# Retention's outputs and state updates issued in pairs: both halves of a pair behind the turn of y, two state steps per call

## The chip, the cores and the metric

The kernel runs on one core of a Trainium2 chip. The metric is the device time of one execution in microseconds. The kernel before took 1388.43 us, the median of three runs (1386.64 to 1389.92).

## What is computed

One layer of a diffusion backbone over 1024 latent tokens and 256 context tokens of width 1024: a modulated RMS norm, one input projection whose columns feed two mixers (bidirectional chunkwise retention with 4 heads, differential attention with 4 heads), an output projection with a gated residual, then a gated MLP with a width 3 convolution, a second residual and a final norm. The change touches retention alone, which the reference states as

```python
    def step(S, inp):
        qc, kc, vc = inp
        scores = jnp.einsum('bhid,bhjd->bhij', qc, kc) * intra
        o = (jnp.einsum('bhij,bhje->bhie', scores, vc)
             + jnp.einsum('bhid,bhde->bhie', qc * q_dec[..., None], S))
        S = S * c_dec[:, None, None] + jnp.einsum('bhjd,bhje->bhde', kc * k_dec[..., None], vc)
        return S, o
...
    for d in range(2):
        def orient(t):
            return jnp.flip(t, axis=2) if d == 1 else t
...
        o_c, s_c = retention_chunked(qc, kc, vc, log_gamma[d], s0)
        o_l, _ = retention_chunked(ql, kl, vl, log_gamma[d], s_c)
        ret_lat = ret_lat + head_group_norm(orient(o_l), gn_g[d])
...
    y_ret_lat = jax.nn.silu(rg_l) * ret_lat.astype(dtype)
```

Chunks have 128 tokens, so a head has 8 chunks of latent tokens and 2 of context, walked forward (d = 0) and backward (d = 1); each chunk's output needs the state S that has come to it from its side.

## The kernel before

The large products are written in three passes: each float32 operand is split into a high part and a remainder, both in the type fp32r, and `passes` (L128 to L133) issues high by high, high by low, low by high. On TensorE that is an endless stream of 128x512 matmuls with lines L131, L132 and L133. Retention's own products are 128x128 in plain float32 and are issued **between** these passes; the trace shows each of them as two MATMUL instructions.

The mixing is done by generators. `natural` and `transposed` (the projections) call `tick` after every k, that is after three passes, and `tick` adds a rate to a counter and calls `next` on the generator that stands beside the projection whenever the counter reaches 1. So a `yield` in the generator is a place where the stream of passes goes on, and what is written between two yields is issued as one group.

Two generators matter. `states((0, 1))` stands beside the projection of block 3 (rate 21/62): it forms the states of heads 0 and 1. A head takes 10 steps, `one` in the code, forward and backward in turn. One step loads k and v of two chunks (`kvs`, 4 buffers, loaded four steps ahead), scales k by its decay on ScalarE (`ks`, L314, 2 buffers, one step ahead), multiplies on TensorE into the PSUM tile `pu` (L330; one or two products) and folds `pu` into the state on VectorE (`S`, L336 and L338). `outputs()` stands beside blocks 0 and 4 (rate 1.35). It walks over 16 pairs of chunks, four of each head. Iteration n loads pair n + 2, scores pair n + 1 (`pc` on TensorE, L254; `sc` on VectorE, L256; `qq` on GpSimd, L251), computes the two halves of pair n's output (`po`, L262 and L263: for each half two directions of scores times v plus q times S), copies and squares it on ScalarE (`o`, `jk`, `ss`), normalises pair n - 1 on VectorE (`o`, L278) and gates it on GpSimd (`y`, L280 and L281), and turns y of pair n - 3 for the output projection (`pyt` on TensorE, L286; `yr` on ScalarE and VectorE; a DMA to `yrd`). An iteration has six yields. In iterations 4 to 11 it also advances the states of heads 2 and 3, five steps in every two iterations.

All small PSUM tiles (`pu`, `pc`, `po`, `pyt`) are taken in the order of the program from one cycle of five banks, `tr_tile`: a tile waits until the tile five places before it has been read.

A scheduler then fixes the order of each engine's instructions; an engine works strictly in that order. Weights of the next block come along with it: `split_slice` (L182) issues a DMA to `raw` on the SyncE queue, casts `whi` on ScalarE (L187) and subtracts `wlo` on VectorE (L188). Block 4's slices pass through the middle of the retention stage. The SyncE queue carries these loads, the loads of k, v and gate (`kvs`, `kvo`) and the stores of `yrd` in one order; a `kvo` load waits until GpSimd has multiplied an earlier pair's y by its gate. At the end, pair 15's y releases GpSimd's loads for attention, `ks` and `qhl` among them, and the first attention scores `pA` (L873) wait for these.

## Time and profile before

| | us |
|---|---|
| median of the three runs | 1388.43 |
| the profiled execution's own time | 1387.15 |
| its span, first to last instruction | 1385.4 |
| TensorE busy in the span | 1363.2 (98%) |
| states of heads 0 and 1 beside block 3 | 273.4 to 318.6 |
| outputs, and states of heads 2 and 3, beside blocks 0 and 4 | about 331 to 428.8 |
| first attention score | 452.2 |

Times in the traces count from the first instruction. The stage that the change touches is thus some 155 us of the span. In rows of the timeline the columns are: start in us, duration in us, engine, line, operation, out<-in, shapes, count of merged instructions, and in brackets the idle time before it and who ended that. A merged row of two matmuls gives the start of the first.

### The profile page before, as it was taken

Reading aid. Unit: us, or ns where it says so; the run is one execution under the profiler, and the core shown is the slowest. Engines: PE = TensorE matmul, PEld = TensorE weight load, DVE = VectorE, ACT = ScalarE, POOL = GpSimd, SP = SyncE. Lnnn points to the kernel's source line nnn. Section 1 sums busy time; section 2 is a strip of 40 time slices with the busy share of each in tenths; the row PEclk is TensorE's granted clock in tenths of the full one; section 3 lists DMA queues with packets and bytes.
Section 4 is the critical chain, followed back from the end, with each engine's and each line's share of the span. In section 5 each row is a group of like instructions: output and inputs, shape, how many; then the busy total and the mean of one; then the engine's idle time right before and its main releaser. Section 6 shows DMA issues by size and latency. Waiting matters only on the chain. (4 is left out here: it accounts for less than half of the span.)

```text
span 1385.4 us, 19442 instructions
## 1 busy us (share of the span) xinstructions
PE 1363.2 (98%) x7042; PEld 1146.0 (83%) x7042; DVE 994.4 (72%) x1469; ACT 732.2 (53%) x1395; POOL 303.6 (22%) x323
## 2 busy tenths in 40 slices
PE   8999999999999999999999999999999999999997
PEld 6788888888988799998888788888888888888886
DVE  4655773424676898895458997788778877798757
ACT  4652322434675789987136654555545555454543
POOL 1310000002655424411200643222332220000001
PEclk9999999999999999999999999999999999999999
DMA  9546885454565778622410232332323325963523
GB/s 373 202 168 210 296 267 184 145 176 144 155 188 151 208 179 182 139 48 99 172 65 23 99 115 99 114 114 94 112 101 112 113 71 174 373 227 106 175 92 129
DMA packets 94759, 214.61 MB, mean 155 GB/s; under 512 B 9220, under 2 KB 29188, under 8 KB 94152
## 3 DMA queue, kind: packets, MB, share of 16 engines
q1 hardware_dynamic: 85928, 186.90, 39.2%
q0 software_dynamic: 8160, 24.91, 7.9%
q10 hardware_dynamic: 576, 1.57, 0.3%
q8 instruction: 55, 0.90, 0.3%
q14 instruction: 40, 0.33, 0.1%
HBM read 158.03 MB, written 55.31 MB: 154 GB/s over the span
## 5 line engine op out<-in xcount | busy, mean ns | idle before, releaser
L131 PE MATMUL pl<-hT,whi 128*128 128x512 f32 x256 | 105.8, 413 | 0.0
L131 PE MATMUL chain<-T,whi 128*128 128x512 f32 x264 | 103.0, 391 | 1.2 <-ACT ub L1298 0.9
L132 PE MATMUL chain<-T,whi 128*128 128x512 f32 x264 | 102.8, 389 | 0.0
L133 PE MATMUL chain<-T,wlo 128*128 128x512 f32 x264 | 102.4, 389 | 0.0
L133 PE MATMUL pl<-hT,wlo 128*128 128x512 f32 x256 | 100.2, 391 | 0.0
L132 PE MATMUL pl<-hT,whi 128*128 128x512 f32 x256 | 99.9, 390 | 0.0
L876 DVE TENSOR_REDUCE mt<-pA 128x1 f32<-128x1280 f32 x64 | 95.1, 1489 | 3.0 <-PE pA L873 1.3
L873 PE MATMUL pA<-ks,qhl 128*128 128x512 f32 (+1 forms) x384 | 89.5, 369 | 1.4 <-DMA ks<-dk 1.0
L131 PE MATMUL c<-whi,ghl 128*128 128x512 f32 x232 | 90.2, 389 | 0.0
L132 PE MATMUL c<-wlo,ghl 128*128 128x512 f32 x232 | 90.2, 389 | 0.0
L133 PE MATMUL c<-whi,ghl 128*128 128x512 f32 x232 | 90.2, 389 | 0.0
L880 ACT ACTIVATE p<-pA,mt 128x1280 f32<-128x1280 f32 x64 | 85.5, 1336 | 5.5 <-DVE mt L876 5.4
L1044 ACT CAST whi<-cmb 128x512 fp32r<-128x512 f32 x62 | 38.5, 623 | 80.5 <-PE chain L132 66.3
L873 PEld LDWEIGHTS pA<-ks,qhl 128*128 128x128 f32 x384 | 67.7, 189 | 13.8 <-issue 1.4
L905 PE MATMUL pv<-va,aT 128*128 128x128 f32 x640 | 77.0, 275 | 0.1
L1204 POOL TENSOR_TENSOR cmb<-wrb 128x512 f32<-128x512 f32 x19 | 28.3, 1488 | 221.1 <-DMA wrb<-w_up 168.2
L1047 DVE TENSOR_TENSOR wlo<-cmb,whi 128x512 fp32r<-128x512 f32 x62 | 60.0, 970 | 20.4 <-ACT whi L1044 20.4
L905 PEld LDWEIGHTS pv<-va,aT 128*128 128x128 f32 x640 | 73.9, 192 | 0.7 <-DVE yT L934 0.3
L1044 ACT CAST whi<-wra 128x512 fp32r<-128x512 f32 x55 | 33.9, 623 | 72.9 <-PE third L132 42.3
L133 PE MATMUL third<-yT,wlo 128*128 128x512 f32 x168 | 65.4, 389 | 0.0
L132 PE MATMUL third<-yT,whi 128*128 128x512 f32 x168 | 65.4, 389 | 0.0
L131 PE MATMUL third<-yT,whi 128*128 128x512 f32 x168 | 65.4, 389 | 0.0
(327 smaller groups left out, 3843.0 us busy)
## 6 DMA issues: line engine op xcount, KB each, us to landing
wm<-w_mod SPq DMA_DIRECT2D x32, 512.0 KB, 5.1
raw<-w_in SPq DMA_DIRECT2D x27, 512.0 KB, 4.7
wra<-w_up SPq DMA_DIRECT2D x24, 512.0 KB, 3.3
wrb<-w_up SPq DMA_DIRECT2D x22, 512.0 KB, 3.5
W<-w_down SPq DMA_DIRECT2D x44, 256.0 KB, 5.8
ad<-s SPq DMA_DIRECT2D x20, 512.0 KB, 3.6
wra<-ad SPq DMA_DIRECT2D x20, 512.0 KB, 3.7
kvs<-kvg SPq DMA_DIRECT2D x36, 256.0 KB, 3.1
```

What stands on the lines that cost most here:

```text
L131: mm(ps, lh, rh, start=first, stop=False, skip_group_check=more)
L132: mm(ps, lh, rl, start=False, stop=False, skip_group_check=more)
L133: return mm(ps, ll, rh, start=False, stop=last, skip_group_check=more)
L873: mm(self.pa[m][:, c0:c1], self.q[:, m, i, qs], self.k[:, m, c0:c1], start=(i == 0), stop=(i == 1))
L876: nc.vector.tensor_reduce(out=self.mt[:, m : m + 1], in_=self.pa[m][:, :LK], axis=AX.X, op=ALU.min)
L880: nc.scalar.activation(self.p[m], self.pa[m][:, :LK], AF.Exp, scale=-1.0, bias=self.mt[:, m : m + 1], accum_out=self.s[:, m : m + 1])
L905: mm(self.pv, self.aT[:, c, :], self.v[:, c, :], start=(c == 0), stop=(c == NKT - 1))
L1044: cast = nc.scalar.copy(hi, src)
L1047: nc.vector.tensor_tensor(out=lo, in0=src, in1=r32(hi), op=ALU.subtract)
L1204: nc.gpsimd.tensor_tensor(out=s1, in0=b1, in1=b2, op=ALU.add)
```

## The change

- A call of `states` now makes two steps, a forward and a backward one. Two scaled keys are held ahead instead of one, and both are made again behind the second product. The rate beside block 3 goes from 21/62 to 11/62, since there are 11 calls instead of 21.
- In `outputs`, the first half of pair n's output moves from its own yield to the place where y is turned and the second half is made: turn, both halves, squares.
- In iterations 4 to 11 the state generator is called once with the scores, and once more in the middle of iterations 4 and 8. That is again 20 steps by the end of iteration 11.

Nothing is added or removed: each engine has as many instructions, and the SyncE and GpSimd queues as many DMAs. Only their order moves.

```diff
@@ -316,15 +316,13 @@
 
             load_until(4)
             yield
-            ahead = scaled_keys(0)
+            ahead = [scaled_keys(0), scaled_keys(1)]
             for i, (h, d, g, cs) in enumerate(seq):
                 if i % len(one) == 0:
                     states_at[h] = [rt.tile([P, NT, P], F32, name=f"S{e}") for e in range(2)]
                     last, made = [None, None], [-2, -2]
                 load_until(i + 4)
-                kv, ks = kvs[i], ahead
-                if i + 1 < len(seq):
-                    ahead = scaled_keys(i + 1)
+                kv, ks = kvs[i], ahead.pop(0)
                 pu = tr_tile([P, 2, P], "pu")
                 for c in cs:
                     mm(pu[:, c, :], ks[:, c, :], kv[:, 1, c, :], start=True, stop=True)
@@ -337,7 +335,9 @@
                     else:
                         nc.vector.scalar_tensor_tensor(out=dst, in0=last[d], scalar=cd[:, d * H + h : d * H + h + 1], in1=pu[:, c, :], op0=ALU.mult, op1=ALU.add)
                     last[d] = dst
-                yield
+                if i % 2:
+                    ahead += [scaled_keys(j) for j in range(i + 1, min(i + 3, len(seq)))]
+                    yield
 
         def outputs():
             n_pairs, per_head = H * NT // 2, NT // 2
@@ -350,13 +350,13 @@
                 if n + 1 < n_pairs:
                     pairs[n + 1].score()
                 forming = per_head <= n < 3 * per_head
-                if n == per_head - 1 or forming and n % 2 == 0:
+                if n == per_head - 1:
+                    next(more)
+                if forming:
                     next(more)
                 yield
-                if 0 <= n < n_pairs:
-                    pairs[n].output(0)
                 yield
-                if forming:
+                if forming and n % per_head == 0:
                     next(more)
                 yield
                 if n == n_pairs + 2:
@@ -366,13 +366,12 @@
                 elif n >= 3:
                     pairs[n - 3].turn()
                 if 0 <= n < n_pairs:
+                    pairs[n].output(0)
                     pairs[n].output(1)
                     pairs[n].squares()
                 yield
                 if 0 <= n - 1 < n_pairs:
                     pairs[n - 1].gate()
-                if forming:
-                    next(more)
                 yield
                 yield
 
@@ -838,7 +837,7 @@
         tr2 = psb2.enter_context(tc.tile_pool(name="tr2", bufs=2, space=PSUM))
         mm2 = psb2.enter_context(tc.tile_pool(name="mm2", bufs=1, space=PSUM))
         banks.update(mm=itertools.cycle([ps_a, ps_a, mm2]), tr=itertools.cycle([pst] * 3 + [tr2] * 2))
-        beside(states((0, 1)), 21 / 62, 0.7)
+        beside(states((0, 1)), 11 / 62, 0.35)
         natural(wg, lat_lhs, range(NT), store_to(kvg_row(2), func=AF.Silu, c0=NTC))
         wg = stream_block(0)
         beside(outputs(), 1.35, -16.0)
```

What the scheduler made of it is seen at three places. The first is TensorE in iteration 5, from the scores of pair 6 to those of pair 7 (`pc`); `pl` are the passes of the projection. Before:

```order
L254 MATMUL pc_3266<-xa,rk 128x128 x2
L262 MATMUL po<-kvo,sc 128x128
L263 MATMUL po<-S_2656,qq 128x128
L262 MATMUL po<-kvo,sc 128x128
L263 MATMUL po<-S_2657,qq 128x128
L131 MATMUL pl<-hT_168,whi 128x512
L132 MATMUL pl<-hT_170,whi 128x512
L133 MATMUL pl<-hT_168,wlo 128x512
L330 MATMUL pu<-kvs,ks 128x128 x2
L131 MATMUL pl<-hT_168,whi 128x512
L132 MATMUL pl<-hT_170,whi 128x512
L133 MATMUL pl<-hT_168,wlo 128x512
```

```order
L286 MATMUL pyt<-ident,y 128x128 x2
L262 MATMUL po<-kvo,sc 128x128
L263 MATMUL po<-S_2656,qq 128x128
L262 MATMUL po<-kvo,sc 128x128
L263 MATMUL po<-S_2657,qq 128x128
L131 MATMUL pl<-hT_168,whi 128x512
L132 MATMUL pl<-hT_170,whi 128x512
L133 MATMUL pl<-hT_168,wlo 128x512
L330 MATMUL pu<-kvs,ks 128x128 x2
```

(The second fence goes on where the first ends, and three more passes end the iteration.) The same iteration of the changed kernel:

```order
L254 MATMUL pc_3277<-xa,rk 128x128 x2
L328 MATMUL pu<-kvs,ks 128x128 x4
L131 MATMUL pl<-hT_168,whi 128x512
L132 MATMUL pl<-hT_170,whi 128x512
L133 MATMUL pl<-hT_168,wlo 128x512
L131 MATMUL pl<-hT_168,whi 128x512
L132 MATMUL pl<-hT_170,whi 128x512
L133 MATMUL pl<-hT_168,wlo 128x512
L286 MATMUL pyt<-ident,y 128x128 x2
L262 MATMUL po<-kvo,sc 128x128
L263 MATMUL po<-S_2670,qq 128x128
L262 MATMUL po<-kvo,sc 128x128
```

(Six more `po` products and six passes follow.) Four groups with three passes behind each have become two groups with six. Over the whole stage, from the first `pu` to the last `pyt`, the row counts give 76 groups before and 47 now. Before, 35 of them have three passes behind them, 16 have six and 24 have nine or more (one has two); now it is 1, 24 and 22.

The second place is where block 4's last weight slice arrives, in iterations 10 and 11. On ScalarE before, from the turn of pair 7's y (`yr`) on; the first `o` is the copy of pair 10's output:

```order
L290 CAST yr<-pyt 128x256
L429 ACTIVATE xb<-pl 64x512
L267 COPY o<-po 128x512
L187 CAST whi<-raw 128x1024
L271 ACTIVATE jk,ss<-o 128x128
L314 ACTIVATE ks<-kvs,kd 128x256
```

and now:

```order
L290 CAST yr<-pyt 128x256
L428 ACTIVATE xb<-pl 64x512
L187 CAST whi<-raw 128x1024
L267 COPY o<-po 128x512
L271 ACTIVATE jk,ss<-o 128x128 x4
```

The cast of the slice now stands ahead of the copy of pair 10's output. On VectorE at the same place, before (`S` are the state updates, `sc` the scores of pair 12):

```order
L432 TENSOR_TENSOR xb<-xb,rtab_2072 128x512
L338 SCALAR_TENSOR_TENSOR S_3516<-S_3516,cd,pu 128x128
L433 TENSOR_TENSOR xa<-xa,xb 128x512
L188 TENSOR_TENSOR wlo<-raw,whi 128x1024
L338 SCALAR_TENSOR_TENSOR S_3516<-S_3516,cd,pu 128x128
L256 TENSOR_TENSOR sc<-pc_3797,dec 128x512
```

and now:

```order
L336 SCALAR_TENSOR_TENSOR S_3518<-S_3518,cd,pu 128x128
L278 SCALAR_TENSOR_TENSOR o<-o,ss,gn 128x128
L291 TENSOR_TENSOR yr<-pyt,yr 128x256
L430 SCALAR_TENSOR_TENSOR xa<-pl,rtab_2072 128x512
L431 TENSOR_TENSOR xb<-xb,rtab_2072 128x512
L188 TENSOR_TENSOR wlo<-raw,whi 128x1024
L432 TENSOR_TENSOR xa<-xa,xb 128x512
L278 SCALAR_TENSOR_TENSOR o<-o,ss,gn 128x128 x3
L256 TENSOR_TENSOR sc<-pc_3799,dec 128x512
```

The state updates of steps 16 and 17 now all stand ahead of the slice's `wlo`; before, one stood behind it.

The third place is GpSimd a little earlier, where pair 8's y (`y`, two rows) and pair 11's scaled queries (`qq`) meet. Before:

```order
L273 TENSOR_TENSOR ss<-ss,mhalf 128x4
L280 TENSOR_TENSOR y<-o 128x256
L251 TENSOR_TENSOR qq<-xa,qd 128x512
L281 TENSOR_TENSOR y<-y,kvo 128x256
L273 TENSOR_TENSOR ss<-ss,mhalf 128x4
```

and now:

```order
L273 TENSOR_TENSOR ss<-ss,mhalf 128x4
L251 TENSOR_TENSOR qq<-xa,qd 128x512
L280 TENSOR_TENSOR y<-o 128x256
L281 TENSOR_TENSOR y<-y,kvo 128x256
L273 TENSOR_TENSOR ss<-ss,mhalf 128x4
```

The queries of pair 11 no longer split pair 8's y but go ahead of it. The load of `kvo` on the SyncE queue that waits for this y stands directly ahead of the last slice's `raw` load now; before, a `kvs` load stood between them.

## The prediction

> **What bounds the kernel now.** I read the page's head first, then the busy times of the two stretches that hold retention, then TensorE's timeline in them, then what TensorE waits for there.
>
> ```profile
> span 1385.4 us, 19442 instructions
> PE 1363.2 (98%) x7042; PEld 1146.0 (83%) x7042; DVE 994.4 (72%) x1469; ACT 732.2 (53%) x1395; POOL 303.6 (22%) x323
> ...
> 273.40:318.60 45.20, 45.20 (x236) 38.39 (x235) 13.25 (x37) 17.21 (x31) 0.00 (x0) 1.00 0.63 187
> 331.00:428.80 97.80, 97.19 (x634) 86.94 (x634) 66.45 (x152) 60.77 (x196) 58.15 (x56) 1.00 0.45 141
> ```
>
> The last two rows give, for each stretch, its length and then the busy time of TensorE, its weight loads, VectorE, ScalarE and GpSimd, the granted clock, the DMA share and GB/s. TensorE is busy for all of the first stretch and for 97.19 of 97.80 us of the second, at the full clock, while VectorE reaches 68% and the others less. So TensorE sets the end, and the change can save only two things there: what a small group costs beyond its own products, and the 0.6 us and more in which TensorE waits. The products themselves all stay.
>
> **What a group costs beyond its products.** First the pace of each kind alone, by the starts.
>
> ```profile
> 268.75 0.39 PE L133 MATMUL pn<-whi,hT 128*128 128x512 f32 x1
> ...
> 271.70 0.39 PE L131 MATMUL pn<-whi,hT 128*128 128x512 f32 x1
> ...
> 336.97 0.38 PE L262 MATMUL po<-kvo,sc 128*128 128x128 f32 x2
> ...
> 337.64 0.39 PE L263 MATMUL po<-S,qq 128*128 128x128 f32 x2
> 337.78 0.47 PE L131 MATMUL pl<-hT,whi 128*128 128x512 f32 x1
> ```
>
> Between the first two rows lie 13 passes in 2.95 us, 0.227 us each. Between the next two lie six small instructions in 0.67 us, 0.112 each. Now whole cycles, from one group to the next:
>
> ```profile
> 276.89 0.61 PE L330 MATMUL pu<-kvs,ks 128*128 128x128 f32 x4
> 277.25 0.48 PE L131 MATMUL pn<-whi,hT 128*128 128x512 f32 x1
> ...
> 279.41 0.61 PE L330 MATMUL pu<-kvs,ks 128*128 128x128 f32 x4
> ...
> 339.25 0.60 PE L254 MATMUL pc<-xa,rk 128*128 128x128 f32 x4
> ...
> 340.39 0.38 PE L262 MATMUL po<-kvo,sc 128*128 128x128 f32 x2
> ```
>
> From 276.89 to 279.41, 2.52 us, stand four small instructions and nine passes: 4 x 0.112 + 9 x 0.227 = 2.49, so 0.03 us is over. From 336.97 to 339.25, 2.28 us, stand eight and six: 0.89 + 1.36 = 2.25, again 0.03 (0.025 with one digit more). From 339.25 to 340.39, 1.14 us, stand four and three: 0.45 + 0.68 = 1.13, so 0.012. A group of four costs no less than one of eight; what counts is that there is a group, and the surplus is spread over the passes behind it. With 0.012, 0.025 and 0.031 for three, six and nine or more passes, the groups before cost 35 x 0.012 + 16 x 0.025 + 24 x 0.031 = 1.56 us, and those now 1 x 0.012 + 24 x 0.025 + 22 x 0.031 = 1.29 us. **The first term is 0.27 us less.** Merging cannot give more than the whole 1.56.
>
> **The two waits.** These are the only waits of TensorE over 0.25 us between the first `pu` group and the last output.
>
> ```profile
> 405.94 0.39 PE L263 MATMUL po<-S,qq 128*128 128x128 f32 x2
> 406.93 0.46 PE L330 MATMUL pu<-kvs,ks 128*128 128x128 f32 x2 [0.60 <-ACT jk L271]
> 407.14 0.47 PE L131 MATMUL pl<-hT,whi 128*128 128x512 f32 x1
> ...
> 410.19 0.39 PE L262 MATMUL po<-kvo,sc 128*128 128x128 f32 x2
> 410.59 0.49 PE L263 MATMUL po<-S,qq 128*128 128x128 f32 x2
> 410.83 0.48 PE L131 MATMUL pl<-hT,whi 128*128 128x512 f32 x1
> ...
> 401.01 0.59 ACT L267 COPY o<-po 128x512 f32<-128x512 f32 x1
> 404.18 1.05 ACT L187 CAST whi<-raw 128x1024 fp32r<-128x1024 f32 x1 [2.58 <-DMA raw<-w_in]
> ...
> 405.36 1.21 DVE L188 TENSOR_TENSOR wlo<-raw,whi 128x1024 fp32r<-128x1024 f32 x1
> 406.49 0.34 DVE L338 SCALAR_TENSOR_TENSOR S<-S,cd,pu 128x128 f32<-128x128 f32 x1
> ...
> 410.19 0.34 DVE L338 SCALAR_TENSOR_TENSOR S<-S,cd,pu 128x128 f32<-128x128 f32 x1
> ```
>
> A row of two small ones takes 0.22 us to the next small one and 0.14 to a pass (337.64 to 337.78). From 405.94 to the pass at 407.14 are 1.20 us where 0.36 would do: 0.84 lost. From 410.19 to 410.83 are 0.64 where 0.36 would do: 0.28 lost. The profile names a ScalarE square for the first, but `pu` of step 19 takes the PSUM bank of step 17's `pu`, five places back, and the last read of that is the state update that ends at 406.83, 0.1 us ahead of the product. It stands behind `wlo`, which waits for `whi`, which waits for the slice's DMA. In the changed order the updates of steps 16 and 17 stand ahead of `wlo`, and steps 18 and 19 use banks one whole iteration old: this wait goes. The second wait is for the last state of head 3, which pair 12 needs in its first half. That half now comes behind six passes and the turn, and step 19 a half iteration earlier: it goes too. **The second term is 1.12 us less.**
>
> **What is late next: the same slice.** The copy of pair 10's output (401.01) now stands behind the cast that waits for the slice, and pair 11's output takes the bank that this copy frees, since there are now exactly five small tiles an iteration.
>
> ```profile
> 401.41 0.61 PE L254 MATMUL pc<-st,rk 128*128 128x128 f32 x4
> ...
> 394.24 1.58 POOL L280 TENSOR_TENSOR y<-o 128x256 f32<-128x256 f32 x1 [1.83 <-DVE o L278]
> 395.77 2.35 POOL L251 TENSOR_TENSOR qq<-xa,qd 128x512 f32<-128x512 f32 x1
> 398.06 0.74 POOL L281 TENSOR_TENSOR y<-y,kvo 128x256 f32<-128x256 f32 x1
> ...
> 398.83 0.32 SPq L227 DMA_DIRECT2D kvo<-kvg  x1
> 399.24 0.38 SPq L227 DMA_DIRECT2D kvs<-kvg  x1
> 399.68 0.42 SPq L184 DMA_DIRECT2D raw<-w_in  x1
> ```
>
> TensorE comes to pair 11's output at 401.41 + 0.45 (scores) + 0.45 (both `pu`) + 2.07 (nine passes) + 0.22 (turn), less half of the first term: 404.4. The slice's DMA was issued behind a `kvo` load that waited for pair 8's y (ended 398.80), and its cast began 4.50 us after the issue. Queries now go ahead of that y on GpSimd. At best they use the 1.83 us in which it stood idle: y takes its usual 0.74 + 0.74 from 394.24 and ends at 395.8. At worst they take their 2.35 from 394.24 and y its 1.58 + 0.74 behind them: 398.9. With `kvs` gone from between, the issue is some 0.45 us behind y, the cast begins between 400.8 and 403.9, and the copy of `o` ends 1.7 later (1.05 + 0.59 and the hand-over): 402.5 to 405.6. Against 404.4 that is a wait of 0 to 1.2 us. On VectorE the scores of pair 12 also stand behind `wlo`, and pair 13's scores need their bank; at the late end this adds 0.3. Below nothing it cannot go, since it is a new wait. The middle of the range gives none, so I take **0.3 us more** for the third term and keep 0 and 1.5.
>
> **What I cost at nothing.** Two keys ahead instead of one need their loads one step earlier. A buffer is freed a whole period before the keys are scaled, 18 passes and eight small ones, 5.0 us beside block 3, and a load lands in 3.1 (row below); with that cover gone, each of some eighteen groups would wait. The turn stands ahead of both halves, and would hold up eight products; but pair 7's y was there at 388.07, and its turn came at 398.47.
>
> ```profile
> kvs<-kvg SPq DMA_DIRECT2D x36, 256.0 KB, 3.1
> ...
> 387.33 0.74 POOL L281 TENSOR_TENSOR y<-y,kvo 128x256 f32<-128x256 f32 x1
> ...
> 398.47 0.38 PE L286 MATMUL pyt<-ident,y 128*128 128x128 f32 x2
> ```
>
> **Sum.** -0.27 - 1.12 + 0.3 = -1.1 us. The profiled execution took 1387.15 us in all, 1.75 over its span, and would come to 1386.1. It lies 1.28 under the median of the three runs, so for a median I say 1388.43 - 1.1 = **1387.3**.
>
> **Rivals.** *Each change of kind costs more than the starts say.* The first pass behind a group is shown with 0.47 or 0.48 us and the others with 0.39. If these 0.09 us were real, 29 groups fewer would save 2.6, with the waits 3.7: 1384.7, faster. The cycles above speak against it, since they close to 0.03; the long row only starts early, 0.14 us behind the row ahead. The Trainium skill's page "Perfetto Trace Analysis" (section "Tensor Engine Instruction (MATMUL, LD_WEIGHTS)") says that TensorE's reported start is real but its end is computed from the instruction's size, which fits: go by starts. Its page "TensorE: Matmul & The Clock Gate" (section "Single matmul latency") gives a lone matmul a fixed 398 cycles at 2.4 GHz, 0.166 us, that a stream hides; if every change of kind laid that bare, 29 fewer would save an estimated 4.8 us, but the cycles of this trace show 0.03 a group and not 0.17. Chance 0.1.
>
> *The gain is swallowed at the border to attention.* TensorE waits there already:
>
> ```profile
> 452.21 1.16 PE L873 MATMUL pA<-ks,qhl 128*128 128x512 f32 x4 [1.03 <-DMA ks<-dk]
> ...
> 439.76 0.74 POOL L281 TENSOR_TENSOR y<-y,kvo 128x256 f32<-128x256 f32 x1
> 440.44 2.58 POOL L952 DMA_DIRECT2D qhl<-dq  x4
> 442.98 2.11 POOL L955 DMA_DIRECT2D ks<-dk  x4
> ```
>
> The loads are issued behind pair 15's y. Were that y held by anything but TensorE's last output, TensorE would come earlier and only wait longer: 1388.4. Against it: from pair 14's outputs to `pA` the passes and groups are the same in both orders, and so are ScalarE's rows and GpSimd's; y follows TensorE. Chance 0.13.
>
> *The slice comes late, and TensorE waits longer than before.* Place and price are those of the third term: the wait is the cast's begin + 1.7 - 404.4. It outweighs the 1.39 us gained when the cast begins after 404.1, about where it began before (404.18). If the queries cannot use GpSimd's idle time and y ends 2 us later, at 400.8, the cast begins at 405.8 and the wait is 3.1: 1390.1, slower than before. For it: GpSimd's 2.35 and 1.58 us there are far over the usual 1.32 and 0.74. Against it: 1.83 us of idle time just ahead. Chance 0.15; beyond 0.2% only if the cast begins after 406.9.
>
> **Chances.** The forecast has 0.62. About 0.2% of the time, 2.8 us, is what a measurement of this kernel can tell from no change. Faster by more than that is the first rival with a little beside it: 0.12. Slower by more is the far end of the third, or a wait that I have not seen, such as the keys' loads: 0.07. The rest, 0.81, is within. The range reaches from the first rival to the third, 1384.8 to 1390.2.
>
> **What would show it.** Right: no wait of TensorE at the product of step 19 and at pair 12's first half; the same 0.03 us a group; the cast of the last slice at 401 to 404, and pair 11's first `po` right behind its turn. Wrong: whole cycles that no longer close with 0.227 and 0.112; a gap ahead of pair 11's `po` or pair 13's `pc`; gaps ahead of `pu` in each iteration; or a wait ahead of `pA` that has grown by as much as the stage before it has shrunk.

## The result, and the profile after

| | before | after |
|---|---|---|
| median of 20 runs each, us | 1389.84 | 1392.21 |
| profiled execution, us | 1387.15 | 1390.68 |
| its span, us | 1385.4 | 1388.5 |

The ratio after to before is 1.0022, with a 95% interval from 1.0015 to 1.0028. The change makes the kernel 2 to 3 us (0.2%) **slower**: 2.4 us by the medians, 3.1 by the ratio and by the spans. The prediction had 1.1 us faster, and as a time 1387.3, reckoned from a median of three runs that lies 1.4 us under the one of 20. The changed kernel lies 2 us above the upper end of the range, in the part that had a chance of 0.07.

Not all of it lies in the span: from the span to the whole time are 2.09 to 2.25 us in the changed kernel's executions and 1.72 to 1.85 in those of the kernel before. No run tells why, and what follows is about the other 3 us. One execution in each of three of the later kernels took 1709 to 5174 us; the ratios leave these out, and the medians of those kernels would be at most 0.5 us lower without them.

First the head of the page after, and the two stretches again (length, then busy time of TensorE, its weight loads, VectorE, ScalarE, GpSimd, then clock, DMA share, GB/s). The second stretch ends 1.8 us later, as the outputs do.

```profile
span 1388.5 us, 19462 instructions
PE 1363.6 (98%) x7042; PEld 1145.6 (83%) x7042; DVE 992.3 (71%) x1469; ACT 731.3 (53%) x1395; POOL 304.7 (22%) x323
...
273.40:318.60 45.20, 45.20 (x235) 38.53 (x234) 13.10 (x36) 17.11 (x30) 0.00 (x0) 1.00 0.60 185
331.00:430.60 99.60, 97.03 (x635) 86.97 (x636) 66.64 (x152) 60.34 (x194) 59.00 (x56) 1.00 0.45 144
```

TensorE's work is the same to 0.4 us. In the second stretch it stands still for 2.57 us, where it had been 0.61. Where that is, its timeline shows:

```profile
275.70 1.05 PE L328 MATMUL pu<-kvs,ks 128*128 128x128 f32 x8
...
280.03 1.05 PE L328 MATMUL pu<-kvs,ks 128*128 128x128 f32 x8
...
330.20 0.39 PE L133 MATMUL pl<-hT,wlo 128*128 128x512 f32 x1
331.59 0.71 PE L254 MATMUL pc<-st,rk 128*128 128x128 f32 x4 [1.00 <-DVE st L432]
332.05 0.48 PE L131 MATMUL pl<-hT,whi 128*128 128x512 f32 x1
...
405.01 0.38 PE L286 MATMUL pyt<-ident,y 128*128 128x128 f32 x2
407.37 0.49 PE L262 MATMUL po<-kvo,sc 128*128 128x128 f32 x2 [1.98 <-ACT o L267]
407.69 0.39 PE L263 MATMUL po<-S,qq 128*128 128x128 f32 x2
...
412.48 0.38 PE L286 MATMUL pyt<-ident,y 128*128 128x128 f32 x2
412.70 0.39 PE L262 MATMUL po<-kvo,sc 128*128 128x128 f32 x2
...
454.32 1.40 PE L872 MATMUL pA<-ks,qhl 128*128 128x512 f32 x6 [0.90 <-DVE xhl L416]
...
464.73 0.50 PE L872 MATMUL pA<-ks,qhl 128*128 128x512 f32 x1 [0.89 <-ACT p L879]
```

The reader is to see four things. A whole cycle of the longer groups still closes: from 275.70 to 280.03, 4.33 us, stand eight small instructions and fifteen passes, 0.90 + 3.40 = 4.30. Pair 12's first half follows its turn at once (412.48, 412.70): the two old waits are gone. In their place pair 11's output waits: from 405.01 to 407.69 are 2.68 us where 0.44 would do, 2.25 lost without rounding. And pair 0's scores wait for the turned queries: from 330.20 to 332.05 are 1.85 us where 0.59 would do, 1.26 lost, against 0.21 before.

I compare the kernels by a **lag**: how much later than before TensorE begins the same product. At the first pass of block 3 it is -0.05 us (267.56 against 267.61), at the 61st product of probabilities and values, in the fourth attention unit, +3.20 (492.41 against 489.21); from there on it stays. (For all kernels the lag is taken less what it is at block 3's first pass, since in 5 of 15 traced executions, of different kernels, TensorE had 0.83 of its clock in the first 20 us and was 2.2 us later from there on; by it a median of some ten runs can be off by a microsecond.) A lag is read from one execution of a kernel; where it and the medians differ by some 2 us, as in two kernels below, neither is exact. The 3.25 us between come in this way:

| from | to | lag grows by | with |
|---|---|---|---|
| block 3's first pass | block 0's first pass | -0.47 | ten groups fewer; a wait of 0.17 less behind a transpose |
| there | pair 4's scores | +1.19 | pair 0's scores, 1.05 of it |
| there | the last output | +1.11 | pair 11's output +2.25, the two old waits -1.12 |
| there | the last turn of y | +0.46 | y of pairs 14 and 15 |
| there | the first attention score | -0.13 | |
| there | the fourth attention unit | +1.09 | ScalarE's exponentials (464.73) |

Why pair 11's output waits is read backwards from ScalarE's copy of pair 10's output. ScalarE after, with both of the slices that matter:

```profile
327.20 1.05 ACT L187 CAST whi<-raw 128x1024 fp32r<-128x1024 f32 x1 [3.19 <-DMA raw<-w_in]
328.28 1.20 ACT L428 ACTIVATE xb<-pl 64x512 f32<-64x512 f32 x2
...
389.42 0.51 ACT L314 ACTIVATE ks<-kvs,kd 128x256 f32<-128x256 f32 x1 [2.90 <-DMA kvs<-kvg]
389.84 0.56 ACT L267 COPY o<-po 128x512 f32<-128x512 f32 x1
...
394.33 0.28 ACT L272 ACTIVATE ss<-ss,geps 128x4 f32<-128x4 f32 x1
...
405.79 1.04 ACT L187 CAST whi<-raw 128x1024 fp32r<-128x1024 f32 x1 [3.89 <-DMA raw<-w_in]
406.74 0.58 ACT L267 COPY o<-po 128x512 f32<-128x512 f32 x1
```

The SyncE queue after:

```profile
384.76 0.32 SPq L227 DMA_DIRECT2D kvo<-kvg  x1
...
385.65 1.34 SPq L227 DMA_DIRECT2D kvs<-kvg  x3
...
401.66 0.32 SPq L227 DMA_DIRECT2D kvo<-kvg  x1
402.07 0.38 SPq L184 DMA_DIRECT2D raw<-w_in  x1
```

GpSimd after, and the one row of VectorE beside its y:

```profile
394.69 1.06 POOL L273 TENSOR_TENSOR ss<-ss,mhalf 128x4 f32<-128x4 f32 x1 [4.85 <-ACT ss L272]
395.73 1.29 POOL L251 TENSOR_TENSOR qq<-xa,qd 128x512 f32<-128x512 f32 x1
398.04 2.78 POOL L280 TENSOR_TENSOR y<-o 128x256 f32<-128x256 f32 x1 [1.02 <-DVE o L278]
400.90 0.73 POOL L281 TENSOR_TENSOR y<-y,kvo 128x256 f32<-128x256 f32 x1
...
397.88 2.35 DVE L188 TENSOR_TENSOR wlo<-raw,whi 128x1024 fp32r<-128x1024 f32 x2
```

And before, the copy of pair 8's output on ScalarE and the same two remainders on VectorE:

```profile
386.46 0.59 ACT L267 COPY o<-po 128x512 f32<-128x512 f32 x1 [0.40 <-PE po L263]
...
394.01 1.22 DVE L188 TENSOR_TENSOR wlo<-raw,whi 128x1024 fp32r<-128x1024 f32 x1
...
395.73 1.22 DVE L188 TENSOR_TENSOR wlo<-raw,whi 128x1024 fp32r<-128x1024 f32 x1
```

Iteration 8 has two state calls, so the keys of steps 14 and 15 are made half an iteration after those of 12 and 13. The loads for them go out at 385.65, when the call before has freed their buffers, and the last key waits for them until 389.42. The copy of pair 8's output stands behind that key: 389.84, where it had been 386.46. Of these 3.4 us the key's wait gives 1.8; for the other 1.6 TensorE itself is later with the last product of that output (387.67 instead of 386.10), behind the extra call. The copy's squares now meet the projection's `xb` and a slice's cast, and `ss` ends at 394.6 instead of 391.3. So y of pair 8 comes when VectorE works on two remainders back to back: its addition takes 2.78 us where it took 1.58 before, beside one remainder, and 0.74 beside none, and y ends at 401.63 instead of 398.80. The `kvo` load waits for it, the slice's load stands behind `kvo` (402.07 instead of 399.68), the cast waits for the slice (405.79 instead of 404.18), and the copy of pair 10's output for the cast.

### The profile page after: what moved, and what is told of

The parts are those of the page before. It is cut to its first block, busy times and chain, and to the rows that moved or that the text cites. A ratio compares the mean times of both kernels' runs of the same rounds, so it can differ in the third digit from the quotient of the medians.

```text
span 1388.5 us, 19462 instructions
## 1 busy us (share of the span) xinstructions
PE 1363.6 (98%) x7042; PEld 1145.6 (83%) x7042; DVE 992.3 (71%) x1469; ACT 731.3 (53%) x1395; POOL 304.7 (22%) x323
```

## The experiments

All kernels were timed beside the kernel before; the differences between medians in the text are against the median of before of the same occasion (1388.79 to 1389.59). "Lost" is the time beyond the pitch of the rows, as for the two waits above; a bracket leaves out the start of a row's first instruction and shows some 0.26 us less. `order_only(a, b)` puts instruction a behind b on their engine, with no wait of its own.

| kernel | median, us | ratio to before (95%) | lag, us |
|---|---|---|---|
| the changed kernel | 1392.21 | 1.0022 (1.0015 to 1.0028) | 3.25 |
| states in pairs alone | 1391.95 | 1.0018 (1.0008 to 1.0029) | 3.12 |
| outputs together alone | 1386.57 | 0.9987 (0.9979 to 0.9996) | -1.13 |
| outputs, and states in pairs beside block 3 | 1387.07 | 0.9987 (0.9978 to 0.9996) | 0.16 |
| outputs, and states in pairs in iterations 4 to 11 | 1392.22 | 1.0019 (1.0010 to 1.0028) | 3.86 |
| changed, copy ahead of the last cast | 1391.98 | 1.0019 (1.0010 to 1.0028) | 3.86 |
| changed, copy ahead of the last cast, first slice later | 1389.65 | 1.0006 (0.9996 to 1.0016) | 2.37 |
| changed, `kvo` on GpSimd's queue | 1391.67 | 1.0015 (1.0006 to 1.0024) | 1.32 |
| changed, extra calls later | 1394.40 | 1.0028 (1.0017 to 1.0038) | 5.15 |
| changed, last slice's load early | 1389.54 | 1.0009 (1.0000 to 1.0018) | |
| the same kernel again | 1391.34 | 1.0018 (1.0008 to 1.0027) | 2.63 |
| changed, last slice's load early, first slice later | 1389.57 | 1.0004 (0.9995 to 1.0014) | 0.23 |
| late pairs, last slice's load early | 1389.74 | 1.0007 (0.9997 to 1.0016) | 3.07 |
| early pairs, first slice later | 1386.70 | 0.9983 (0.9974 to 0.9991) | -2.12 |
| changed, key behind the squares | 1391.52 | 1.0016 (1.0005 to 1.0027) | 1.95 |

### The two halves of the change

**Paired states alone**: pair n's first half goes back to its own yield.

```diff
+                if 0 <= n < n_pairs:
+                    pairs[n].output(0)
                 yield
...
-                    pairs[n].output(0)
                     pairs[n].output(1)
```

> Only the state steps are paired; the first half of each output stays at its own place, as before. Theory A: in this order the copy of pair 8's output does not stand behind a key that waits for its load, and the copy of pair 10's output stands ahead of the last slice's cast, so the wait ahead of pair 11's output is under 0.5 us; pair 0's scores still wait about 1.2 us, since that chain comes from the loads beside block 3. Time: 0.2 below to 1.2 us over the kernel before. A rival C (paired steps alone carry the loss, by the keys' loads needed a step earlier): 2 us or more over the kernel before, with waits ahead of pu.

Measured: 2.6 us over before, the time that I had given to rival C, but not with rival C's waits ahead of `pu` (the one there is loses 0.44 us). Pair 11's output waits for nothing, as theory A had it; but the last slice is late here too (its load goes out at 406.05, in an execution 2.3 us late from the start), and TensorE stands 0.93 us for its remainder `wlo` itself, and then for the scores behind it.

**Outputs together alone**: the kernel before, with the first half moved, and the states left as they were.

```diff
-                if 0 <= n < n_pairs:
-                    pairs[n].output(0)
                 yield
...
+                    pairs[n].output(0)
                     pairs[n].output(1)
```

> Only the outputs are put together (turn, both halves, squares in one group); the state steps stay one a call, as before. Theory A: pair 0's scores wait 0.2 us as before; the last slice's cast stands ahead of the copy of pair 10's output, but the slice itself comes as early as before (cast near 404.2), so pair 11's output waits 0 to 1.5 us; the wait of 0.84 us at step 19's product may stay. Time: 0.8 below to 1.3 us over the kernel before. Rival D (bunched outputs alone carry the loss): 2 us or more over the kernel before.

Measured: **faster**, by 2.7 us in the median, 1.8 by the ratio and 1.13 in the lag; better than either theory's range. The cast of the last slice begins at 402.37, and no wait of TensorE in the outputs' stage is over 0.33 us. So the outputs bring what the prediction had hoped for from the whole change, and the paired states take it away.

Which pairs? The next two are the changed kernel with a flag in `states`, which makes one step a call for one of the two generators, and the calls of before where that is the second.

```diff
-            ahead = [scaled_keys(0), scaled_keys(1)]
+            ahead = [scaled_keys(j) for j in range(2 if two else 1)]
...
+                if not two and i + 1 < len(seq):
+                    ahead = [scaled_keys(i + 1)]
...
+                if not two:
+                    yield
-                if i % 2:
+                elif i % 2:
```

> The outputs together as in the changed kernel, the state steps paired only for heads 0 and 1 (beside block 3); heads 2 and 3 one step a call, as before. Theory A (loads, keys and slices in one queue's order): of the loss of paired steps only the part at pair 0's scores is there: a wait of about 1.2 us instead of 0.2 there and none over 0.4 us in iterations 4 to 12, so 0.8 to 1.3 us over the run with the outputs alone (1386.6), 1387.4 to 1387.9. Rival C (a paired step costs something each time, wherever it is): half of the 5.6 us between the two kernels, 1389 or more.

> The outputs together as in the changed kernel, the state steps paired only for heads 2 and 3 (iterations 4 to 11); heads 0 and 1 one step a call. Theory A: pair 0's scores wait 0.2 us as before; the wait ahead of pair 11's output, or one of the same size at the last slice's wlo, is there (1.5 to 2.3 us), and the border to attention loses another 0.5 to 1.5; 2 to 4.5 us over the run with the outputs alone: 1388.6 to 1391.1. Rival C: half of the loss, about 1389.4, spread over many groups and not in one or two waits.

Measured: the pairs beside block 3 cost 0.2 us in the median beside the outputs alone, nothing in the ratio and 1.3 us in the lag; the pairs of iterations 4 to 11 cost 5.4 us (5.0 in the lag). With the early pairs the time is below the 1387.4 to 1387.9 that I gave; pair 0's scores lose 0.85 us, and step 19's product some 0.7, where I had expected no wait over 0.4. With the late pairs it is above 1391.1, and the border takes nothing (a lag of 3.98 at the last turn of y, 3.86 at the fourth unit), where I had expected 0.5 to 1.5. Most of the loss is in the late pairs, and there in one wait. TensorE there, and then four stretches of which two are shown (columns as above):

```profile
407.22 0.41 PE L286 MATMUL pyt<-ident,y 128*128 128x128 f32 x2
410.25 0.49 PE L262 MATMUL po<-kvo,sc 128*128 128x128 f32 x2 [2.62 <-ACT o L267]
```

```profile
410.40:412.40 2.00, 2.00 (x15) 2.00 (x16) 2.00 (x6) 1.87 (x10) 0.07 (x1) 0.76 0.76 257
412.40:414.60 2.20, 2.20 (x8) 1.81 (x8) 2.20 (x5) 0.64 (x2) 2.12 (x3) 0.50 0.03 9
```

Rival C is out: the loss isn't spread over the groups (before that wait the lag is 0.60, and 0.55 was lost at one late key). With the start of its first instruction the wait costs 2.9 us, some 0.6 more than in the changed kernel. TensorE does not come earlier: without the 2.2 us from the start, both kernels reach that turn within 0.03 us of each other. The slice comes later, its cast at 408.66, 0.6 us later than in the changed kernel when the start is taken off. Behind the wait TensorE runs at half its clock for some 3 us, which costs another 1.6.

### Is it the copy behind the cast?

The cast is ordered behind the copy of pair 10's output, as before the change.

```diff
-            nc.scalar.copy(whi, raw)
+            cast = nc.scalar.copy(whi, raw)
+            if behind is not None:
+                order_only(cast.ins, behind.ins)
```

> The changed kernel with one ScalarE order turned back: the cast of block 4's last slice stands behind the copy of pair 10's output, as in the kernel before. Theory A (the loss is made of a few places where small work stands behind a cast that waits for a slice's DMA): the wait of 2.25 us ahead of pair 11's output goes, a wait of at most 0.4 us may come later in the same iteration because wlo stands ahead of the scores, and the time falls by 1.8 to 2.2 us below the changed kernel, to about the time of the kernel before or 0.4 over it. Theory B (the longer groups themselves, or outputs that come in one piece, keep TensorE waiting somewhere in each iteration): the wait only moves to another row, and less than 1 us is won.

```profile
410.18 0.49 PE L133 MATMUL pl<-hT,wlo 128*128 128x512 f32 x1 [0.53 <-DVE wlo L190]
411.04 0.71 PE L258 MATMUL pc<-st,rk 128*128 128x128 f32 x4 [0.37 <-DVE sc L260]
```

Nothing is won: 1391.98. The wait of 2.25 us is gone, and TensorE waits three rows on for the slice itself, then for scores that VectorE makes behind it. In this execution the slice itself came 2.0 us later than in the changed kernel's (cast at 407.82 instead of 405.79; the key of iteration 8 waited 3.78 us instead of 2.90), so its rows alone can't price the copy's place, but the median of eleven executions can. Theory A's first form, that the *place* of the copy costs the time, falls. What is left of A is that the slice is late. Theory B's number came true for another reason than its own.

The same, with **block 4's first slice** behind the first turned queries (cast behind the second `xb`, remainder behind the sum `st`):

```diff
+            for ins, other in zip((cast, low), behind):
+                order_only(ins.ins, other.ins)
```

> As the run with the copy ahead of the last slice's cast, and also block 4's first slice (cast and remainder) behind the first turned queries of block 0. Theory A: the wait ahead of pair 0's scores falls from 1.26 to about 0.2 us, which gives another 0.8 to 1.1 us over the other run, 2.6 to 3.3 us below the changed kernel and 0.2 to 0.9 below the kernel before; some 1 us stays lost at the border to attention. Theory B: no more than the other run, within 0.3 us of it.

Measured: 1389.65, 1.5 us of lag less than without it. The wait at pair 0's scores falls from 1.26 to 0.17 us. That is the +1.05 of the table, and more than the 0.3 that theory B allowed; below the kernel before, as I had expected, it isn't.

### Is it the load's place in the queue?

First all `kvo` loads on GpSimd's own queue, where nothing stands behind a load that waits for y.

```diff
-            nc.sync.dma_start(out=kv, in_=kvg_d[g][:, h, s0 : s0 + 2])
+            q.dma_start(out=kv, in_=kvg_d[g][:, h, s0 : s0 + 2])
```

> The changed kernel with one thing else: the kvo loads, which wait for y on GpSimd, are issued on GpSimd's own queue instead of SyncE's, so that the kvs loads and the slice's load no longer stand behind them. Theory A: the keys of iteration 8 are there in time, pair 8's y comes at about 399 again, the last slice's cast begins before 404, and the wait ahead of pair 11's output falls under 0.5 us; the wait at pair 0's scores stays at about 1.2. Time 1.5 to 3 us under the changed kernel, 1389.2 to 1390.7; if the issues themselves hold GpSimd up by more than 0.6 us each, half of that is given back. Theory B: no change, within 0.5 us of the changed kernel.

Measured: no wait ahead of pair 11's output, and a lag of 1.32; but the median is only 0.3 us nearer to the kernel before than the changed kernel's is, where I had expected 1.5 to 3. The traced execution lost 1.5 us near the end of the kernel, far from the change; whether the others did is not on record, so the gain is shown for the stage and not for the kernel. No key is late here, and still y of pair 8 ends at 403.71 (401.5 without the 2.2 us from the start), not at 399: the slice is early (its load at 401.20, or 399.0) because its load no longer waits for that y.

Then the sharpest one: on the SyncE queue the slice's load goes ahead of the one `kvo` load that waits for pair 8's y; no other row of any engine moves.

```diff
+            load = nc.sync.dma_start(out=raw, in_=src)
+            if ahead_of is not None:
+                order_only(ahead_of.ins, load.ins)
```

> The changed kernel with one DMA in another place on the SyncE queue: the load of block 4's last slice goes ahead of the kvo load that waits for pair 8's y, and of nothing else; no other engine's order moves. The lag is how much later than the kernel before TensorE comes to the fourth attention unit, less the lag that it has at the first product of block 3; for the changed kernel it is 3.25 us. Theory A (the slice is late because its load stands behind that kvo load): the load now waits only for its buffer, which the remainder of the slice two before frees at about 399; the cast begins by 403.5 instead of 405.8, the wait ahead of pair 11's output falls from 2.25 to under 0.4, and the lag to between 0.6 and 1.6 us; time 1389.5 to 1390.7. Rival E (the late y of pair 8 holds TensorE anyway, through the bank, the gates or the turn): the wait moves to another row and the lag stays over 2.5.

> The same kernel as the run with the last slice's load ahead of the kvo load, once more, for its trace: the one taken before shows TensorE at a small part of its clock for almost the whole span and says nothing of the stage. Theory A, with the two other kernels that have this load early as a guide: cast of the last slice at 402.5 to 403.5, a wait of less than 0.6 us ahead of pair 11's output, 1.26 us still ahead of pair 0's scores, lag between 0.8 and 1.8 us.

Measured: 1389.54, inside the range, and 1391.34, outside it, with intervals that overlap. Of the first one's trace I had said that TensorE is at a small part of its clock; its passes are over 1 us apart, but the clock on record is 1.00, and the reason isn't known. In the second the cast begins at 404.21, pair 11's output waits for nothing, and the scores of pair 13 wait instead:

```profile
406.01 0.41 PE L293 MATMUL pyt<-ident,y 128*128 128x128 f32 x2
406.26 0.39 PE L269 MATMUL po<-kvo,sc 128*128 128x128 f32 x2
...
410.24 0.71 PE L261 MATMUL pc<-st,rk 128*128 128x128 f32 x4 [0.64 <-DVE sc L263]
```

The lag, 2.63, misses my range: the 2.25 us are gone, but 0.90 come back at those scores and 0.94 at two products of this execution that wait for a late key (0.55 and 0.39), and the border takes 1.0, as in the changed kernel. The key of iteration 8 came later still (a wait of 3.92 us), so the load had to wait for its buffer until 400.59, where I had reckoned with 399. What rival E forecast, a wait on another row and a lag over 2.5, is what this execution shows; whether the late y is behind it, as E says, is not shown, for the scores wait on VectorE, and what made them late there isn't separated. For the changed kernel alone, then, the runs don't show that this one load is worth its 2.25 us. The same load was moved in two other kernels, one with the first slice's edit, one with late pairs alone:

> The early load of the last slice, and also block 4's first slice (cast and remainder) behind the first turned queries of block 0. Theory A: both big waits of the changed kernel go (1.26 at pair 0's scores to about 0.2, 2.25 at pair 11's output to under 0.6); the lag falls to between -0.5 and 0.8 us and the time to 1388.5 to 1389.8, that of the kernel before or a little less, but still 1 to 2 us over the outputs alone. Rival E: the lag stays over 1.5.

> The outputs together, the state steps paired for heads 2 and 3 alone, and the load of the last slice ahead of the kvo load. Without that place of the load the lag was 3.9 us, with a wait of 2.88 us ahead of pair 11's output and several passes at half pace 5 us later. Theory A: the wait falls under 0.6, the slow passes go with it, and the lag falls to between -1 and 0.5 us; time 1387 to 1389. If the slow passes have a cause of their own, they stay and the lag is 1 us more.

Measured: with both slices in order the changed kernel is level with the one before (1.0004, interval 0.9995 to 1.0014), lag 0.23, and no wait ahead of the border is over 0.6 us. With the late pairs alone the one moved load takes the lag at the last turn of y from 3.98 to 0.02 us; the half clock behind pair 11's output goes with the wait. Both executions are 2.2 us late from the start, so their rows compare directly. The queue and ScalarE without and with it:

```profile
404.36 0.32 SPq L227 DMA_DIRECT2D kvo<-kvg  x1
404.77 0.38 SPq L184 DMA_DIRECT2D raw<-w_in  x1
...
408.66 1.04 ACT L187 CAST whi<-raw 128x1024 fp32r<-128x1024 f32 x1 [3.55 <-DMA raw<-w_in]
```

```profile
401.11 0.33 SPq L184 DMA_DIRECT2D raw<-w_in  x1
403.66 0.32 SPq L232 DMA_DIRECT2D kvo<-kvg  x1
...
404.78 1.05 ACT L189 CAST whi<-raw 128x1024 fp32r<-128x1024 f32 x1 [1.59 <-DMA raw<-w_in]
```

The lag of 3.07 at the fourth attention unit, far over my 0.5, comes behind that: in this execution the first `pA` stood 2.59 us for the load of `ks`, and TensorE lost its clock there. That product began 8.5 us after the last issue of these loads on GpSimd had ended, where it had been 7.1 before the change; no run tells why. Most executions must have lost less: the median, 1389.74, is 1 us over the kernel before and 0.7 over what I expected.

### Why pair 8's y is late

The extra calls moved to iterations 7 and 11:

```diff
-                if forming and n % per_head == 0:
+                if forming and n % per_head == per_head - 1:
                     next(more)
```

> The changed kernel with the extra call of the state generator in iterations 7 and 11 instead of 4 and 8, so that no iteration near the last slice's load has two calls. Theory A: the copy of pair 8's output does not wait behind a key whose load comes late, y of pair 8 ends before 400, the last slice's cast begins by 404.5 and pair 11's output waits under 0.6 us; the wait of 1.2 us at pair 0's scores stays. Time 1 to 2.5 us under the changed kernel, 1389.7 to 1391.2. Against it: steps 8 and 9 come a half iteration ahead of pair 8's output, and a key may now be late there. Theory B: no change, within 0.5 us.

```profile
406.37 0.39 PE L133 MATMUL pl<-hT,wlo 128*128 128x512 f32 x1
410.83 1.38 PE L328 MATMUL pu<-kvs,ks 128*128 128x128 f32 x4 [4.08 <-DVE o L278]
```

Measured: 1394.40, a miss. The copy of pair 8's output waits for no key, and its y ends at 402.53 in an execution that is 2.2 us late from the start, so 1.3 us earlier than in the changed kernel. But the extra call now falls into iteration 11, behind the slice: its keys stand on ScalarE behind the cast (407.12) and pair 10's squares, the first is made at 410.29, and the product follows at 410.83. The profile names VectorE; ScalarE's key is what ended last. This wait is the run's own, and so long that TensorE loses its clock too.

Then the key alone, ordered behind the squares of pair 8's output:

```diff
+                if (self.h, self.g) == (2, 0):
+                    order_only(keys[3, 15].ins, square.ins)
```

> The changed kernel with the key of step 15 behind the squares of pair 8's output on ScalarE (the product of step 15 goes with it, three passes later); the order of the slice's load and the kvo load stays as changed. Theory A, first half of the chain (the key that waits 2.9 us for its load holds up pair 8's output, and so its y): the copy of that output comes at about 387 instead of 389.8, its y ends at 398 to 400 instead of 401.6, the last slice's cast begins at 402.5 to 404, and the wait ahead of pair 11's output falls from 2.25 to under 0.8; lag 0.8 to 2.2 us. Rival F (y of pair 8 is late by VectorE's or GpSimd's own order, whatever the key does): y still ends after 401 and the wait stays over 1.8.

```profile
405.74 0.38 PE L288 MATMUL pyt<-ident,y 128*128 128x128 f32 x2
406.38 0.49 PE L262 MATMUL po<-kvo,sc 128*128 128x128 f32 x2 [0.26 <-ACT o L267]
```

Measured: y of pair 8 ends at 400.35 instead of 401.63, the cast begins at 404.80 instead of 405.79, the wait falls from 2.25 to 0.53 us lost, the lag to 1.95. The key is a cause of the late y, and not the only one: the copy comes 1.8 us earlier, y only 1.3, since GpSimd still shares that time with VectorE's remainders (last section). The times of copy, y and cast stay outside what I had expected, the cast by 0.8 us; the moved key itself now keeps its product waiting, 0.67 us at 392.72. Rival F is out. In the ratio (1.0016 against 1.0022) the gain can't be told from none.

### The best version

The kernel with early pairs, and the first slice's edit from above:

> The outputs together, the state steps paired beside block 3 alone, and block 4's first slice behind the first turned queries. Theory A: the wait of 0.85 us at pair 0's scores falls to about 0.2 and nothing else moves: the lag falls from 0.2 to between -1.2 and -0.4 us, time 1386 to 1387, the lowest or second lowest of all. Against it: TensorE comes earlier to the state product of step 19 (0.67 us) and to the border, which may give the gain back.

```profile
329.67 0.71 PE L258 MATMUL pc<-st,rk 128*128 128x128 f32 x4
...
450.11 1.39 PE L882 MATMUL pA<-ks,qhl 128*128 128x512 f32 x6
```

Measured: 1386.70, ratio 0.9983 (0.9974 to 0.9991), the lowest ratio of all. Pair 0's scores and the first attention score wait for nothing that the profile shows; the lag of -2.12 is 0.9 us better than I had expected, and that is the border's wait (1.03 us before). Whether it beats the outputs alone the intervals don't tell.

## Why the prediction was wrong, step by step

- *"The first term is 0.27 us less"*: right as far as it can be seen. Beside block 3, where nothing else waits, ten groups fewer gave 0.47 us, 0.17 of it at a transpose; 0.30 is left, 0.03 a group. The rival that each change of kind costs 0.09 us is out.
- *"The second term is 1.12 us less"*: right. Both waits are gone.
- *"0.3 us more for the third term"*: **this step failed**. The mechanism is the one described, place included; the size was 2.25 us against bounds of 0 and 1.5. The bounds began y of pair 8 at 394.24, where it stood before, and asked only what GpSimd's queries would do to it. In fact the queries kept out of the way (395.73 to 397.02), and y was late from ahead: its output was copied 3.4 us later, and its addition then met both remainders. (The terms of TensorE's arrival add up to 404.5 and not 404.4; nothing hangs on it.)
- *"What I cost at nothing: two keys ahead"*: this is where that lateness comes from. It gives 1.8 of the 3.4 us; the other 1.6 are TensorE's own, which the forecast of y left out too. The cover was reckoned beside block 3, with a period of 5.0 us and a load of 3.1. The same rule in iteration 8, which has two calls, was not reckoned: its loads went out at 385.65, behind a `kvo` load, and the key waited 2.90 us. TensorE never waits for that key in this trace. What waits is what stands behind it on ScalarE.
- *The third rival, "the slice comes late"*, with a chance of 0.15, is what happened. Its formula gives 405.79 + 1.7 - 404.4 = 3.1 us; TensorE came 0.8 us later than 404.4, so 2.25 were left. The reason it gave, queries on GpSimd, is not what made y late.
- No term of mine had *pair 0's scores*, +1.05 us. It is the same chain one stage earlier. Before, the last load of block 0 and the first of block 4 went out back to back from 319.52; now a load of `kvs` and a store that waits for ScalarE's gate come between, the second goes at 322.23, and its cast, still ahead of the turned queries, is at 327.20 instead of 325.68. I had followed the order of the last slice through the queue, and not that of the first.
- *The border* did not swallow a gain, there was none. It took another 1.0 us in the profiled execution, at the exponentials of the first units, a term that the sum did not have. Its cause stays open. It is not simply the lateness: kernels that came later to the last turn of y lost less behind it (3.40 us late, 0.46 lost; 3.98 late, nothing lost), and over all kernels the border gave or took between 1.1 us less and 3.05 more than before.
- *"1.75 over its span"*, taken for constant, is some 0.4 us more in the changed kernel (first section); the cause is open too.

## What to carry to other kernels

When work on in-order engines is bunched, ask of every load that the bunch needs one step sooner what stands *behind* its first user, and follow that to the next big transfer in the same DMA queue; the engine that uses the load may never wait. A rule for "loads come in time" must be reckoned at the densest place of the schedule, not at the regular one. And an order is best repaired where the chain is longest: moving the copy only moved the wait, while moving the one load took it away in the kernel with late pairs, and in the changed kernel did so together with the first slice.

## What the runs showed of the hardware

**A wait of 2.6 us costs TensorE its clock, and where it falls counts.** In the kernel with late pairs the outputs after an idle time of 2.62 us begin at the usual pace, and 1.2 us later the clock is 0.50, passes 0.43 us apart instead of 0.227, for 3.4 us. An idle time of 2.59 at the border and one of 4.08 (the run with the extra calls later) did the same; the 1.98 us of the changed kernel did not. The Trainium skill's page "TensorE: Matmul & The Clock Gate" (section "What's actually happening") gives half the clock after an idle window of about 3.4 us, counted in windows that run freely. The traces agree on the half and on the windows: with late pairs the granted clock changes at 12.07, 18.90, 411.43 and 414.85 us, which are 2, 115 and 1 times 3.413 us apart. They differ on the threshold: in the windows just ahead of the three drops TensorE was idle for 2.23, 2.41 and 3.02 of the 3.41 us, and not for all of it. The changed kernel's wait fell across a border of two windows, 1.52 us in the first, and the clock stayed full; so it did after up to 1.55 us at the border to attention. In the first 20 us of a kernel a wait of 1.84 to 1.88 us at 10.4 halved the clock in five traces, and one of up to 1.85 did not in the others. By these numbers the limit lies near half a window, so that a wait of some 2 us can cost another 1.6 by where it happens to fall.

**GpSimd and VectorE hold each other up.** The addition of pair 8's y takes 0.74 us alone and 2.78 beside the two remainders of VectorE (398.04 and 397.88 above). The other way round, in the kernel with the key behind the squares, GpSimd came first:

```profile
395.52 1.48 POOL L251 TENSOR_TENSOR qq<-xa,qd 128x512 f32<-128x512 f32 x1 [1.53 <-PE po L263]
396.95 1.72 POOL L282 TENSOR_TENSOR y<-o 128x256 f32<-128x256 f32 x1
398.76 1.59 POOL L283 TENSOR_TENSOR y<-y,kvo 128x256 f32<-128x256 f32 x1
```

```profile
395.75 4.01 DVE L188 TENSOR_TENSOR wlo<-raw,whi 128x1024 fp32r<-128x1024 f32 x2
```

The same two remainders took 4.01 us instead of 2.35. The Trainium skill's page "SBUF — State Buffer" (section "SBUF: two separate sides") says that an instruction of VectorE with two inputs in SBUF and one of GpSimd take a shared pair of ports in turn, each for its whole length; this trace agrees. The kernel before shows it as well: its remainders at 394.01 and 395.73 stand beside the 1.58 us of that y's addition and the 2.35 us of the queries, which are 0.74 and 1.32 elsewhere. The prediction saw that these two were long, used them for its late bound, and did not ask which remainders a later y would meet.
